# Hybrid SSD, attention and convolution trunk: the rows of ones of queries and keys come with a transfer, and a pool of tiles has 50 buffers instead of 52

## The chip, the cores and the metric

The kernel runs on one core of a Trainium2 chip. The metric is the time of one execution on the device in microseconds; lower is better. The core has a matrix engine (TensorE, PE in the profile, with its loads of the stationary operand as PEld), VectorE (DVE), ScalarE (ACT), GpSimd (POOL), and SyncE (SP), whose queue issues nearly all DMA transfers. Each engine executes its own list of instructions in order, and waits where an instruction needs another engine's result or a buffer that is still in use.

## The reference, cut to what matters

Two layers over 512 tokens of width 1024 in float32. The first has an input projection, 16 SSD heads, 16 heads of forgetting attention, and an output projection; the second is a gated convolution module. What bears on the change is the attention:

```python
c = jnp.cumsum(log_f, axis=1)
...
logits = jnp.einsum('bqhp,bkhp->bhqk', qi, k).astype(jnp.float32) * scale
logits = logits + jnp.transpose(cqi, (0, 2, 1))[..., None] - ck[:, :, None, :]
logits = jnp.where(kpos[None, :] <= qpos[:, None], logits, -jnp.inf)
w = jax.nn.softmax(logits, axis=-1).astype(v.dtype)
return jnp.einsum('bhqk,bkhp->bqhp', w, v)
```

To the product of query and key (64 elements each) the cumulated sum c of the query's token is added, and that of the key's token is subtracted.

## The kernel before, in words

All matrix products work on 32-bit values that are split into a high and a low part, each product being the sum of high times high, high times low and low times high. Weights come from memory as 512 KB pieces into the buffers `wr`, are split on ACT (high part) and on DVE or POOL (low part), and are used by a list of jobs (the class `Job`) in a fixed order; one job makes 128 columns of a projection. The low parts of some of the second layer's weights are made ahead, during the first layer: a piece is loaded (tile `pre`, line 202), its high part copied on ACT (line 211), the low part made on DVE (line 212), and stored to memory (line 216).

Beside the jobs, the class `Steps` deals out the work of the SSD heads and of the attention between a job's matmuls; a step is due when the steps that it needs are done for a stated number of microseconds of modelled TensorE time. TensorE's order is thus written out by hand. The other engines' order, and that of the transfers, is made by the compiler's list scheduler from priorities and modelled times.

Tiles come from pools. The pool `t` (line 54) holds tiles of 128 x 512 elements of 4 bytes; nearly all intermediate values live in it, among them `uh` and `ul` (the normed input, two parts), the four tiles of each attention head, the softmax's rows `pr`, the values `vhl`, and the sums `os`. A new tile of a full pool waits until an older one has been read for the last time.

The attention of a head h works on four tiles, which `qk_proj` makes when the projection of queries or keys is in PSUM (64 rows for each of two heads):

- `QS`: the high part of the query in rows 0 to 63 (ACT, line 610), the low part in rows 64 to 127 (DVE, line 611).
- `QX`: the high part again in rows 0 to 63 (a transfer from `QS`, line 612), and four more rows, 64 to 67: two of ones and two with the parts of the cumulated sum.
- `KS`: the high part of the key, twice (ACT, line 623, and a transfer, line 625).
- `KX`: the low part of the key in rows 0 to 63 (DVE, line 624), and four rows, 64 to 67: the two parts of the negative cumulated sum, and two of ones.

The logits of 128 queries (the step `sa`) are the matmul of QS with KS, that of the first 68 rows of QX with KX, and the mask. Then come the row maximum `nmx` on DVE (line 1503), the exponential into `pr` on ACT, the reciprocal of the row sum `ri` on DVE (line 1508), and the product of both on POOL (line 1509). In the step `sb` TensorE transposes `pr` into `pT`, and the transposed rows are split into `ph` and `pl`; the step `sc` multiplies them with the values.

The four additional rows come in two steps: POOL fills rows 64 to 67 with ones (lines 613 and 626), and a transfer from `chl` overwrites two of them (lines 614 and 627). The tile `chl` holds the cumulated sums: rows 32 to 47 of the 16 heads, as high part `csh` and low part `csl`, and the same, negated, in rows 64 to 79 (lines 1216 to 1220).

Of the kernel before, what the change touches and what calls it, by code (L numbers as in the profile page):

```python
# [9 lines left out]
F32R = mybir.dt.float32r  # L10
BF16 = mybir.dt.bfloat16
AF = mybir.ActivationFunctionType
ALU = mybir.AluOpType
# [3 lines left out]
S = 512  # L17
# [19 lines left out]
def trunk(  # L37
# [6 lines left out]
    nc = tc.nc  # L44
    V, G, A, T = nc.vector, nc.gpsimd, nc.scalar, nc.tensor
# [3 lines left out]
    cp = ctx.enter_context(tc.tile_pool(name="const", bufs=1))  # L49
# [1 line left out]
    ep = ctx.enter_context(tc.tile_pool(name="early", bufs=4))  # L51
    eh = ctx.enter_context(tc.tile_pool(name="earlyh", bufs=2))
    qp = ctx.enter_context(tc.tile_pool(name="q", bufs=7))
    tp = ctx.enter_context(tc.tile_pool(name="t", bufs=52))
    hp = ctx.enter_context(tc.tile_pool(name="spill", bufs=8, space=bass.MemoryType.DRAM))
    lop = ctx.enter_context(tc.tile_pool(name="los", bufs=64, space=bass.MemoryType.DRAM))
    sp = ctx.enter_context(tc.tile_pool(name="small", bufs=8))
# [15 lines left out]
    def t2(s, dt=F32):  # L73
        return tp.tile([P, S], dt, tag="t", name=nm(s))
# [10 lines left out]
    def f32(t):  # L85
        return t.bitcast(F32)
# [431 lines left out]
    def fm_job(w, c0, evac, uh, ul, eng=None):  # L518
        def go(wh, wl):
            pb = bank("m")  # L520
            yield from fm_chunks(pb, P, wh, wl, uh, ul)
            evac(pb)
        return Job(w, 0, KT, c0, P, go, eng)
# [80 lines left out]
    def qk_proj(j):  # L604
        def evac_q(pq):
            for s in range(2):
                h = 2 * j + s
                src = slice(64 * s, 64 * s + 64)
                QS, QX = t2("QS", F32R), t2("QX", F32R)
                A.mul(QS[0:64, :], pq[src, :], 0.125)  # L610
                V.scalar_tensor_tensor(QS[64:128, :], pq[src, :], 0.125, f32(QS)[0:64, :], ALU.mult, ALU.subtract)
                nc.sync.dma_start(f32(QX)[0:64, :], f32(QS)[0:64, :])
                G.memset(f32(QX)[64:68, :], 1.0)
                nc.sync.dma_start(f32(QX)[66:68, :], f32(chl)[32 + h : 33 + h, :, :])
                qk["q", h] = (QS, QX)
                done["q", h] = now[0]

        def evac_k(pk):
            for s in range(2):
                h = 2 * j + s  # L620
                src = slice(64 * s, 64 * s + 64)
                KS, KX = t2("KS", F32R), t2("KX", F32R)
                A.copy(KS[0:64, :], pk[src, :])
                V.tensor_tensor(KX[0:64, :], pk[src, :], f32(KS)[0:64, :], ALU.subtract)
                nc.sync.dma_start(f32(KS)[64:128, :], f32(KS)[0:64, :])
                G.memset(f32(KX)[64:68, :], 1.0)
                nc.sync.dma_start(f32(KX)[64:66, :], f32(chl)[64 + h : 65 + h, :, :])
                qk["k", h] = (KS, KX)
                done["k", h] = now[0]
        fm_job(e_w_in, C_Q + j * P, evac_q, uh, ul)  # L630
        fm_job(e_w_in, C_K + j * P, evac_k, uh, ul)
# [581 lines left out]
        V.tensor_tensor(stk[0:16, :], spl[0:16, :], ee[0:16, :], ALU.mult)  # L1213
        act(stk[96:112, :], cs[0:16, :], AF.Exp)

    chl = cp.tile([80, 2, S], F32R, name="chl")
    csh, csl = chl[:, 0, :], chl[:, 1, :]
    A.copy(csh[0:48, :], cs)
    V.tensor_tensor(csl[0:48, :], cs, f32(csh)[0:48, :], ALU.subtract)
    V.tensor_scalar(chl[64:80], f32(chl)[32:48], -1.0, None, ALU.mult)  # L1220

    cs2 = cp.tile([P, S], F32R, name="cs2")
    sel2 = cp.tile([P, 16], F32R, name="sel2")
# [423 lines left out]
```

## Time and profile before

| | before |
|---|---|
| median of 3 runs | 916.59 us (916.2 to 918.29) |
| the profiled execution | 917.41 us, its span 915.6 us |
| granted TensorE clock, mean | 0.994 |
| PE busy | 888.8 us (97%) |
| DVE busy | 711.5 us (78%) |
| ACT busy | 613.2 us (67%) |
| POOL busy | 508.7 us (56%) |
| moved by DMA | 170.32 MB |

All times inside an execution are counted from the start of its span. An engine's idle time is put down to the instruction that ended it, the releaser; `A <- B: 1.1, 1, 1.1` in a table of waits says that A waited for B for 1.1 us in total, once, the longest 1.1. In a list in order of time each row has start and duration in us, engine, line, operation and tiles, and in brackets the idle time just before it with its releaser. In the tables of stages each engine has its busy time and its number of instructions, and at the end stand the granted clock of TensorE, the mean busy share of the 16 DMA engines, and GB/s.

### The profile page before, as it was taken

The page shows a single profiled execution, that of the slowest core. Times are in us where ns is not written, and L with a number is a line of the kernel's source. Part 1 is how long each engine was busy: PE and PEld are TensorE (multiplying, and loading weights), DVE is VectorE, ACT ScalarE, POOL GpSimd, SP SyncE. Part 2 cuts the span into 40 slices and gives each one's busy share as a digit, 9 for nine tenths or more (in the row PEclk, how much of TensorE's full clock was granted, in tenths as well). Part 3 has the DMA queues.
Part 4 walks back from the last instruction along what each step waited for, and adds up shares of the span by engine and source line. Part 5 has one row for each costly group of instructions (what it writes and reads, how often), then busy time and mean ns, then how long its engine had stood idle before and what let it go on. Part 6 is the DMA issues. An engine that isn't in the chain of part 4 may idle for free. (4 is left out here: it accounts for less than half of the span.)

```text
span 915.6 us, 13920 instructions
## 1 busy us (share of the span) xinstructions
PE 888.8 (97%) x4603; PEld 747.9 (82%) x4603; DVE 711.5 (78%) x1270; ACT 613.2 (67%) x1159; POOL 508.7 (56%) x478
## 2 busy tenths in 40 slices
PE   6999999999999999999999999999999999999997
PEld 6888888887889888888678889888888887787885
DVE  5667959788975877869887258999999999889402
ACT  6767587677766776767775538787876959558300
POOL 2723665526443353344743214898999999747310
PEclk9999999999999999999999999999999999999999
DMA  7726523348775585865768993565574754544502
GB/s 211 234 78 216 157 74 88 98 155 256 240 254 174 174 278 163 264 211 173 251 209 301 328 356 103 163 190 155 185 221 149 226 184 146 177 140 159 184 11 104
DMA packets 185068, 170.32 MB, mean 186 GB/s; under 512 B 8413, under 2 KB 152421, under 8 KB 184997
## 3 DMA queue, kind: packets, MB, share of 16 engines
q1 hardware_dynamic: 184980, 169.44, 57.9%
q8 instruction: 36, 0.59, 0.3%
q14 instruction: 36, 0.29, 0.1%
q10 hardware_dynamic: 16, 0.00, 0.0%
HBM read 133.64 MB, written 31.46 MB: 180 GB/s over the span
## 5 line engine op out<-in xcount | busy, mean ns | idle before, releaser
L102 PE MATMUL m<-uh,w 128*128 128x512 f32 (+1 forms) x1392 | 450.8, 391 | 2.0 <-ACT yT L1441 0.8
L102 PEld LDWEIGHTS m<-uh,w 128*128 128x128 f32 x1392 | 260.3, 189 | 51.0 <-ACT yT L1441 1.2
L102 PE MATMUL m<-ul,w 128*128 128x512 f32 (+1 forms) x696 | 266.9, 384 | 0.0
L191 POOL TENSOR_TENSOR w<-wr,w 128x512 fp32r<-128x512 f32 x112 | 159.2, 1446 | 141.9 <-ACT w L159 104.6
L989 DVE SCALAR_TENSOR_TENSOR acc<-h,cw,acc 128x490 f32<-128x490 f32 (+13 forms) x274 | 178.8, 725 | 2.7 <-ACT acc L981 2.0
L896 POOL TENSOR_TENSOR acc<-acc,prod 128x507 f32<-128x507 f32 (+9 forms) x124 | 159.5, 1289 | 8.2 <-ACT prod L882 0.7
L102 PEld LDWEIGHTS m<-ul,w 128*128 128x128 f32 x696 | 131.7, 189 | 21.7 <-issue 0.5
L102 PE MATMUL o<-w,hlh 128*128 128x512 f32 x448 | 140.9, 396 | 0.0
L212 DVE TENSOR_TENSOR pre<-pre,prh 128x512 fp32r<-128x512 f32 x104 | 92.7, 916 | 23.9 <-ACT prh L211 23.1
L102 PEld LDWEIGHTS o<-w,hlh 128*128 128x128 f32 x448 | 82.9, 190 | 15.7
L102 PE MATMUL tm<-w,uh 128*128 128x256 f32 (+1 forms) x384 | 93.3, 334 | 0.0
L159 ACT CAST w<-wr 128x1024 fp32r<-128x1024 f32 x72 | 75.0, 1050 | 20.5 <-DMA wr<-in_e_w_in_dram 7.7
L102 PE MATMUL o<-w,hll 128*128 128x512 f32 x224 | 87.7, 392 | 0.0
L1509 POOL TENSOR_SCALAR pr<-pr,ri 128x128 f32<-128x128 f32 (+1 forms) x64 | 39.7, 621 | 85.6 <-DVE ri L1508 61.8
L882 ACT ACTIVATE prod<-h,cw 128x507 f32<-128x507 f32 (+9 forms) x124 | 79.0, 709 | 0.0
L211 ACT CAST prh<-pre 128x512 fp32r<-128x512 f32 x104 | 62.0, 622 | 16.8 <-DVE pre L212 14.8
L351 POOL TENSOR_TENSOR rstd<-var,mhalf 128x1 f32<-128x1 f32 (+1 forms) x20 | 12.9, 643 | 107.9 <-DVE var L349 83.0
L157 ACT CAST w<-wr 128x1024 fp32r<-128x1024 f32 x56 | 57.2, 1050 | 17.9 <-DMA wr<-in_o_w_out_dram 11.0
L102 PEld LDWEIGHTS tm<-w,uh 128*128 128x128 f32 x384 | 65.0, 196 | 4.7
L102 PE MATMUL tm<-w,ul 128*128 128x256 f32 (+1 forms) x192 | 62.2, 324 | 0.0
L95 ACT ACTIVATE pr<-s,nmx 128x128 f32<-128x128 f32 (+1 forms) x64 | 33.9, 530 | 37.1 <-DVE nmx L1503 21.2
L102 PEld LDWEIGHTS o<-w,hll 128*128 128x128 f32 x224 | 42.3, 189 | 9.1
(265 smaller groups left out, 1537.7 us busy)
## 6 DMA issues: line engine op xcount, KB each, us to landing
wr<-in_e_w_in_dram SPq DMA_DIRECT2D x56, 512.0 KB
lo<-pre SPq DMA_DIRECT2D x52, 512.0 KB
pre<-in_o_w_in_dram SPq DMA_DIRECT2D x48, 512.0 KB
wr<-in_o_w_in_dram SPq DMA_DIRECT2D x48, 512.0 KB
w<-lo SPq DMA_DIRECT2D x48, 512.0 KB
wr<-in_e_w_out_dram SPq DMA_DIRECT2D x16, 512.0 KB
wr<-in_o_w_out_dram SPq DMA_DIRECT2D x16, 512.0 KB
x<-in_x_dram SPq DMA_DIRECT2D x12, 256.0 KB
```

Of the source, the lines that this page charges most:

```text
L95: i = A.activation(*a, **kw)
L102: T.matmul(o, l, r, start=start, stop=stop, skip_group_check=True)
L157: last_cast[0] = A.copy(hi, src).ins
L159: last_cast[0] = A.copy(hi, src).ins
L191: j.eng.tensor_tensor(hl[1][i][:, sl], src[:, sl], f32(hl[0][i])[:, sl], ALU.subtract)
L211: A.copy(h, t[:, sl])
L212: V.tensor_tensor(t.bitcast(F32R)[:, sl], t[:, sl], f32(h), ALU.subtract)
L351: mark["rstd"] = G.tensor_tensor(r, v, mhalf.to_broadcast([P, ss.shape[-1]]), ALU.pow).ins
L882: A.activation(prs[i][:, s:], hs[j][:, : S - s], AF.Copy, scale=w31(30 - s, j))
L896: G.tensor_tensor(a2[j][:, s:], a2[j][:, s:], prs.pop(i)[:, s:], ALU.add)
L989: V.scalar_tensor_tensor(a[:, s:], h[:, : S - s], w31(30 - s, j), a[:, s:], ALU.mult, ALU.add)
L1509: G.tensor_scalar(p[:, :L], p[:, :L], ri, 1.0, ALU.mult, ALU.mult)
```

## The change

The tile `chl` gets two more rows of 512 for each partition, so that it is 80 x 4 x 512. POOL fills it with ones once. The parts of the cumulated sums stand in its rows 2 and 3 in partitions 0 to 47, the negated ones in rows 0 and 1 of partitions 64 to 79. Partition 32 + h thus holds ones, ones, high, low, and partition 64 + h negative high, negative low, ones, ones. One transfer brings all four rows to QX or KX, and the 32 memsets of rows 64 to 67 are gone. The four kilobytes that `chl` needs more in each partition are two buffers of the pool `t`.

```diff
-    tp = ctx.enter_context(tc.tile_pool(name="t", bufs=52))
+    tp = ctx.enter_context(tc.tile_pool(name="t", bufs=50))
...
                 nc.sync.dma_start(f32(QX)[0:64, :], f32(QS)[0:64, :])
-                G.memset(f32(QX)[64:68, :], 1.0)
-                nc.sync.dma_start(f32(QX)[66:68, :], f32(chl)[32 + h : 33 + h, :, :])
+                nc.sync.dma_start(f32(QX)[64:68, :], f32(chl)[32 + h : 33 + h, :, :])
...
                 nc.sync.dma_start(f32(KS)[64:128, :], f32(KS)[0:64, :])
-                G.memset(f32(KX)[64:68, :], 1.0)
-                nc.sync.dma_start(f32(KX)[64:66, :], f32(chl)[64 + h : 65 + h, :, :])
+                nc.sync.dma_start(f32(KX)[64:68, :], f32(chl)[64 + h : 65 + h, :, :])
...
-    chl = cp.tile([80, 2, S], F32R, name="chl")
-    csh, csl = chl[:, 0, :], chl[:, 1, :]
+    chl = cp.tile([80, 4, S], F32R, name="chl")
+    G.memset(f32(chl), 1.0)
+    csh, csl = chl[:, 2, :], chl[:, 3, :]
     A.copy(csh[0:48, :], cs)
     V.tensor_tensor(csl[0:48, :], cs, f32(csh)[0:48, :], ALU.subtract)
-    V.tensor_scalar(chl[64:80], f32(chl)[32:48], -1.0, None, ALU.mult)
+    V.tensor_scalar(chl[64:80, 0:2], f32(chl)[32:48, 2:4], -1.0, None, ALU.mult)
```

## The prediction

> **What bounds the kernel now.** I read the page's first part, then stages of the span, then who TensorE waited for, then the changed tiles. In the page each engine has its busy time, share and instructions:
>
> ```profile
> span 915.6 us, 13920 instructions
> PE 888.8 (97%) x4603; PEld 747.9 (82%) x4603; DVE 711.5 (78%) x1270; ACT 613.2 (67%) x1159; POOL 508.7 (56%) x478
> ```
>
> TensorE (PE) is busy for 888.8 of 915.6 us, so an edit that takes no matmul away can win at most the 26.8 us of idle time, plus what a lowered clock costs. Where these lie is in the busy time by stage (us of the stage; its length, then PE, PEld, DVE, ACT, POOL; granted clock; DMA share):
>
> ```profile
> 0.00:28.00 28.00, 18.60 (x125) 17.00 (x125) 15.93 (x39) 17.21 (x39) 9.29 (x29) 1.00 0.68 199
> 100.00:260.00 160.00, 155.40 (x846) 133.73 (x845) 137.23 (x244) 114.05 (x206) 83.91 (x61) 0.98 0.51 156
> 248.00:256.00 8.00, 8.00 (x44) 8.00 (x43) 8.00 (x15) 5.12 (x10) 2.64 (x3) 0.57 0.56 178
> 260.00:390.00 130.00, 130.00 (x795) 111.12 (x794) 98.38 (x201) 91.17 (x211) 54.53 (x75) 1.00 0.70 217
> 390.00:400.00 10.00, 8.63 (x68) 7.80 (x67) 7.70 (x18) 5.94 (x17) 5.61 (x8) 1.00 0.62 177
> 436.00:440.00 4.00, 1.72 (x8) 0.89 (x8) 3.21 (x8) 1.82 (x5) 1.38 (x4) 0.99 1.00 340
> 440.00:444.00 4.00, 4.00 (x15) 3.12 (x15) 2.72 (x10) 2.74 (x10) 2.39 (x5) 0.58 0.59 234
> 444.00:480.00 36.00, 34.73 (x187) 27.48 (x186) 29.27 (x55) 29.09 (x62) 23.20 (x24) 1.00 0.67 216
> 480.00:820.00 340.00, 339.98 (x1607) 283.78 (x1606) 288.89 (x504) 238.31 (x421) 247.69 (x211) 1.00 0.62 204
> 820.00:840.00 20.00, 18.48 (x80) 14.68 (x79) 20.00 (x31) 16.10 (x26) 11.30 (x7) 1.00 0.38 131
> 909.30:915.60 6.30, 0.01 (x1) 0.00 (x0) 2.17 (x4) 0.69 (x2) 0.55 (x1) 0.90 0.22 85
> ```
>
> 9.4 us are idle before 28 us and 6.3 after 909.3, at the two ends. The heads of queries and keys, which the change touches, run from 260 to about 480 us; there PE stands still for 1.37 us (390 to 400), 2.28 (436 to 440) and 1.27 (444 to 480), 4.9 us together. Two stretches run at a lower clock though PE is busy in all of them: 8 us at 0.57, worth 8 x 0.43 = 3.4 us, and 4 us at 0.58, worth 1.7 us. Each follows idle time; the second stands right behind the 2.28 us. The whole stage thus holds 4.9 + 1.7 = 6.6 us that could be won. Whom PE waited for in it, in us, times, longest (the two ranges 380 to 400 and 420 to 440):
>
> ```profile
> PE pT L106 <- POOL pr L1509: 1.1, 1, 1.1
> PE pT L106 <- ACT pr L95: 1.3, 1, 1.3
> PE s L102 <- ACT pr L95: 1.0, 1, 1.0
> ```
>
> All three are steps of the softmax, none is QX or KX or a transfer.
>
> **The change part by part.** The changed tiles first (duration ns min/median/max, first and last start), then what SyncE's queue waited for POOL:
>
> ```profile
> L613 POOL MEMSET QX<- x16: 518/520/523, 268.2 to 428.0; 4x512 f32 x16
> L612 SPq DMA_DIRECT2D QX<-QS x16: 469/510/1562, 268.9 to 431.2; - x16
> L614 SPq DMA_DIRECT2D QX<-chl x16: 606/629/681, 269.4 to 431.8; - x16
> L626 POOL MEMSET KX<- x16: 518/519/522, 269.2 to 444.1; 4x512 f32 x16
> L627 SPq DMA_DIRECT2D KX<-chl x16: 593/628/669, 273.5 to 445.7; - x16
> L102 PE MATMUL s<-KX,QX x64: 270/309/400, 279.8 to 461.3; 68*128 68x128 f32 x16, 68*128 68x256 f32 x16, 68*128 68x384 f32 x16, 68*128 68x512 f32 x16
> ...
> SPq L627 <- POOL KX L626: 9.8, 6, 3.8
> SPq L614 <- POOL QX L613: 8.0, 5, 2.0
> ```
>
> *32 memsets go.* 16 x 0.520 + 16 x 0.519 = 16.6 us of POOL. POOL is busy 54.53 of 130 us in 260 to 390, and PE's one wait for POOL there is for pr, which itself waits for the reciprocal on DVE. Worth 0 on the path; what hides it is PE, busy for all of the 130 us.
>
> *32 transfers no longer wait for POOL.* SyncE's queue loses 9.8 + 8.0 = 17.8 us of waiting. Behind the waiting instruction stand the loads of weights and of the pieces for the second layer, and the stores of the low parts. PE waits for none of these between 260 and 480, so they come earlier for nothing: 0. Late next is the tile itself: a transfer that opens QX or KX must still wait for a free buffer, now on SyncE instead of POOL.
>
> *The transfers carry four rows instead of two.* 32 x 4 KB more is nothing beside 170 MB. The time to issue one: two rows take 0.63, 64 rows 0.51 us, so four lie at 0.51 to 0.68 (the longest of the two-row ones). I take 0.63, nearest in rows: 32 issues stay at 20.1 us of the queue. From the first of these transfers (269.4) to the first matmul on it (279.8) are 10.4 us, for keys 6.3 (273.5); a transfer that is later by its whole issue time is still in time. 0.
>
> *chl doubles and gets a memset.* 80 x 2048 elements on POOL. The start as it is (start, us, then idle time before it):
>
> ```profile
> 2.53 0.52 POOL L442 MEMSET keep<- 48x512 f32 x1
> 3.60 0.52 POOL L1224 MEMSET cs<- 128x512 f32 x1
> 5.49 0.56 POOL L351 TENSOR_TENSOR rstd<-var,mhalf 128x1 f32<-128x1 f32 x1 [1.34 <-DVE var L349]
> 7.67 0.56 POOL L351 TENSOR_TENSOR rstd<-var,mhalf 128x1 f32<-128x1 f32 x1 [1.62 <-DVE var L349]
> 20.96 1.05 ACT L159 CAST w<-wr 128x1024 fp32r<-128x1024 f32 x1 [3.81 <-DMA wr<-in_e_w_in_dram]
> 23.70 0.36 PE L102 MATMUL m<-uh,w 128*128 128x256 f32 x1 [0.71 <-DVE bm L502]
> ```
>
> 512 elements take 0.52 us whatever the partitions (48 x 512 of keep as well as 128 x 512 of cs), so 2048 take 4 x 0.52 = 2.1 us. The memset of cs stands late in the program and runs at 3.60, where POOL is free; the new one needs as little and will run there too. Then the first rstd starts at about 4.1 + 2.1 = 6.2 instead of 5.49, at most 0.7 us late; the second, at 7.67 behind 1.62 us of idle time, moves by a few tenths. This ends at 20.96: ACT waits 3.81 us there for a weight's transfer, and PE stands 0.71 us before the matmuls fed by it, so the start is set by that transfer. Bounds 0 and +0.7; I take 0, since 0.71 covers the larger. The three other operations on chl keep their sizes, and the first of them follows the scan that makes the cumulated sums, long after the memset.
>
> *Two buffers fewer in the pool t (52 to 50).* This is the one part that takes something from the path. Rows that show the pool at its limit:
>
> ```profile
> 331.24 0.52 POOL L613 MEMSET QX<- 4x512 f32 x1 [2.77 <-DVE QS L611]
> 380.42 0.52 POOL L613 MEMSET QX<- 4x512 f32 x1 [3.47 <-DVE QS L611]
> L1509 POOL TENSOR_SCALAR pr<-pr,ri x64: 374/588/1685, 281.3 to 465.1; 128x128 f32<-128x128 f32 x16, 128x256 f32<-128x256 f32 x16, 128x384 f32<-128x384 f32 x16, 128x512 f32<-128x512 f32 x16
> L588 ACT CAST vhl<-tm x16: 363/378/405, 256.4 to 404.0; 128x256 fp32r<-128x256 f32 x16
> ```
>
> These memsets read nothing and write a fresh tile, yet POOL stands idle 2.77 and 3.47 us for them: they wait until a buffer comes free. How much lead two buffers are: QS, QX, KS and KX make 64 tiles, pr 64, vhl 16, in all 144 from 268 to 465 us, one every 1.37 us. Two buffers are an estimated 2.7 us of lead, wherever the pool is full. KX has 6.3 us of lead and QX 10.4, which covers it; pr is the thin one, since PE already waits for it in 390 to 400 at the end of the full stretch. Lower end 0 (PE idles nowhere in the 130 us in which the two rows lie, with the pool full), upper end +2.7, since a PE that is held back by the lead lost gets that lead back. Tiles that open later also make engines execute in another order (only PE's is written out), which can be worth something of either sign; its bounds are the rivals. I take +0.3, near the lower end, because the 2.77 and 3.47 us of waiting left no mark on PE.
>
> **Sum.** 0 + 0 + 0 + 0 + 0.3. The profiled execution took 917.41 us around its span of 915.6, 0.8 above the median of the runs, 916.59. 917.41 + 0.3 = 917.7 against that execution, 916.6 + 0.3 = 916.9 against the median, which is the forecast.
>
> **Rivals.** *Slower: the pool's loss lands on PE.* Place: 385 to 400 us, where pT waits for pr. It decides if a pr tile's start is put off by more than what is left before its transpose. Price +2.7, so 919.3; if the new stall brings a stretch of low clock, another 1.7 to 3.4, so 921.0 to 922.7. For it: the two slot waits, and PE's wait for pr. Against: 130.00 of 130 in the stage where they lie. [...]
>
> *Faster: the stall at 436 us and the low clock behind it go.* What makes it now:
>
> ```profile
> 432.77 4.08 DVE L212 TENSOR_TENSOR pre<-pre,prh 128x512 fp32r<-128x512 f32 x3
> 436.96 0.42 DVE L1503 TENSOR_REDUCE nmx<-s 128x1 f32<-128x256 f32 x1
> 433.12 3.19 POOL L119 TENSOR_TENSOR hll<-yT,hlh 128x512 fp32r<-128x512 f32 x2 [4.59 <-PE o L102]
> ```
>
> Three subtractions for the second layer run on DVE at 1.36 us each beside a POOL that subtracts too, and the row maximum that PE needs waits behind them. With transfers that reach SyncE earlier, the pieces of those subtractions come at other times; if they leave this place, 2.28 + 1.7 = 4.0 us go: 912.6. With the 1.37 us of 390 to 400 as well, 911.2. Against: the last QX memsets are over 4 us before, so nothing removed stands in this chain.
>
> *The start:* the new memset not hidden, +0.7: 917.3, inside no change.
>
> *The change doesn't do what it says:* SyncE waits for the free buffer for as long as it waited for POOL (the 2.77 and 3.47 us are such waits). 916.6, the same class.
>
> **How the numbers follow.** The forecast with the last two rivals 0.44, the slower one 0.31, the faster one 0.25. A measurement of this kernel can tell about 0.2%, 1.8 us: same is 914.8 to 918.4, the forecast's own range. For 8 in 10 the range takes in the faster rival's 912.6 and the slower one with the smaller dip, 921.0; outside are the double gain and the larger dip.
>
> **What the profile after would show.** Right: no QX or KX memset on POOL, one of about 2.1 us on chl at 3 to 6 us; no wait of the transfers from chl for POOL; QX and KX in time; PE busy 888 to 889 us, 260 to 390 without idle time, and the stalls at 390 to 400 and 436 to 440 about as now. Slower: new waits of pT for pr between 300 and 400, a clock under 0.9 behind them. Faster: 440 to 444 at full clock. Wrong altogether: if the stages from 480 on, or those before 260, changed; DVE, ACT and POOL could be ordered anew there too, and the 3.4 us of low clock at 248 could move, for which I have no row.

## The result, and the profile after

The changed kernel takes 921.77 us (median of 8 runs, 919.25 to 923.83) and the kernel before 917.44 us (8 runs, 915.34 to 919.24). The ratio is 1.0050, with a 95% interval of 1.0035 to 1.0066: slower by 4.3 us. The forecast was 916.9 with a range of 912.6 to 921.0.

The profiled execution took 921.53 us. The first part of its page:

```profile
span 919.8 us, 13860 instructions
PE 890.5 (97%) x4603; PEld 748.8 (81%) x4603; DVE 708.7 (77%) x1270; ACT 613.6 (67%) x1159; POOL 497.0 (54%) x447
```

POOL lost 11.7 us of work (508.7 before): 16.6 us of memsets are gone, the one on `chl` brings 1.8, and its other work takes 3.1 us longer. The span grew by 4.2 us. The same table of stages as before (length, then PE, PEld, DVE, ACT, POOL; granted clock; DMA share; GB/s):

```profile
248.00:256.00 8.00, 8.00 (x55) 8.00 (x56) 8.00 (x14) 5.22 (x9) 2.56 (x3) 0.79 0.55 167
260.00:320.00 60.00, 60.00 (x353) 51.05 (x353) 42.64 (x88) 40.96 (x95) 17.52 (x22) 1.00 0.70 215
320.00:390.00 70.00, 65.23 (x391) 54.97 (x389) 50.55 (x103) 46.63 (x105) 23.30 (x27) 0.98 0.65 202
390.00:400.00 10.00, 8.96 (x74) 8.29 (x72) 7.86 (x20) 7.15 (x20) 5.83 (x7) 1.00 0.68 222
400.00:440.00 40.00, 40.00 (x234) 33.26 (x233) 31.54 (x61) 29.53 (x64) 14.62 (x17) 1.00 0.63 201
440.00:446.00 6.00, 4.13 (x21) 2.64 (x20) 5.01 (x12) 2.88 (x9) 1.77 (x5) 1.00 1.03 353
446.00:450.00 4.00, 4.00 (x16) 3.20 (x15) 2.80 (x9) 2.86 (x9) 1.50 (x3) 0.57 0.11 31
450.00:480.00 30.00, 29.40 (x161) 23.03 (x160) 23.25 (x46) 24.54 (x55) 22.98 (x22) 1.00 0.64 205
480.00:820.00 340.00, 339.98 (x1607) 283.75 (x1606) 288.89 (x504) 238.22 (x420) 244.07 (x210) 1.00 0.63 207
```

From 320 to 390, where PE had no idle time before, it is now idle for 70 - 65.23 = 4.77 us. From 260 to 480 it stands still for 4.77 + 1.04 + 1.87 + 0.60 = 8.3 us, against 4.9 before. From 480 to 820 nothing changed. Since TensorE's order is the same in both kernels, the start of each of its 4603 matmuls can be set against the start of the same matmul before: the lag is +0.07 us at 240, -1.27 at 260 (less low clock at 248), still -1.27 at 320, +5.23 at 350, +4.55 from 480 to 820. The loss of 6.5 us lies between 320 and 350: two waits of 2.75 and 1.84 us, shown below, and an estimated 1.7 us for 3.41 us at half clock behind the second, from 343.61 us. Against it stand 1.3 us won at 248 us, where this execution ran for 3.4 us at half clock and the one before for 6.8, and 0.7 us after 350.

Who PE waited for between 300 and 480 us (in total, times, longest):

```profile
PE pT L106 <- POOL pr L1508: 5.6, 3, 2.7
PE s L102 <- ACT pr L95: 1.0, 1, 1.0
PE pT L106 <- ACT pr L95: 0.9, 2, 0.6
```

The transposes wait for pr on POOL, 5.6 us instead of 1.1. The third of these waits, 1.04 us at 396.77, is as long as the one that was there before. The first, from the lists of DVE, ACT (two rows), POOL (two rows) and PE of the changed kernel:

```profile
319.52 0.69 DVE L1502 TENSOR_REDUCE nmx<-s 128x1 f32<-128x512 f32 x1
321.94 2.00 ACT L159 CAST w<-wr 128x1024 fp32r<-128x1024 f32 x2 [0.33 <-PE o L102]
323.96 0.69 ACT L95 ACTIVATE pr<-s,nmx 128x512 f32<-128x512 f32 x1
323.07 3.51 POOL L191 TENSOR_TENSOR w<-wr,w 128x512 fp32r<-128x512 f32 x2 [2.79 <-ACT w L159]
326.56 1.74 POOL L1508 TENSOR_SCALAR pr<-pr,ri 128x512 f32<-128x512 f32 x1
328.35 0.66 PE L106 MATMUL pT<-ident,pr 128*128 128x128 f32 x4 [2.75 <-POOL pr L1508]
```

and the same place in the kernel before:

```profile
322.56 0.69 ACT L95 ACTIVATE pr<-s,nmx 128x512 f32<-128x512 f32 x1
323.24 1.98 ACT L159 CAST w<-wr 128x1024 fp32r<-128x1024 f32 x2
323.69 0.70 POOL L1509 TENSOR_SCALAR pr<-pr,ri 128x512 f32<-128x512 f32 x1 [1.82 <-issue]
324.36 3.54 POOL L191 TENSOR_TENSOR w<-wr,w 128x512 fp32r<-128x512 f32 x2
326.72 0.60 PE L106 MATMUL pT<-ident,pr 128*128 128x128 f32 x4
```

Two engines changed their order. Before, ACT makes the exponential and then casts two weights; POOL scales pr (0.70 us) and then splits the weights (3.54 us). After, the row maximum is ready at 320.21, but ACT casts the weights first and begins the exponential at 323.96, 3.75 us later. POOL, which gets the cast weights first, splits them first, and pr stands behind 3.51 us of that. PE waits 2.75 us. By the program's tiles and the trace, the buffer of this pr was one that a transpose had just given back at 322.9. This step is a reconstruction: the runs below test the size of the pool and ACT's order, and not this buffer.

At 343 us it happens again (DVE, ACT in three rows, POOL in two, PE):

```profile
334.44 0.42 DVE L1502 TENSOR_REDUCE nmx<-s 128x1 f32<-128x256 f32 x1
336.50 0.48 ACT L95 ACTIVATE pr<-s,nmx 128x256 f32<-128x256 f32 x1 [2.53 <-PE o L102]
338.96 1.05 ACT L159 CAST w<-wr 128x1024 fp32r<-128x1024 f32 x1
339.90 0.69 ACT L95 ACTIVATE pr<-s,nmx 128x512 f32<-128x512 f32 x1
340.09 2.51 POOL L191 TENSOR_TENSOR w<-wr,w 128x512 fp32r<-128x512 f32 x2 [0.65 <-ACT w L159]
342.58 1.03 POOL L1508 TENSOR_SCALAR pr<-pr,ri 128x512 f32<-128x512 f32 x2
343.32 0.89 PE L106 MATMUL pT<-ident,pr 128*128 128x128 f32 x4 [1.84 <-POOL pr L1508]
```

In the kernel before, at this place, pr is scaled first and the cast follows (POOL, then ACT):

```profile
337.95 1.19 POOL L1509 TENSOR_SCALAR pr<-pr,ri 128x512 f32<-128x512 f32 x1 [1.16 <-DVE ri L1508]
339.15 1.05 ACT L159 CAST w<-wr 128x1024 fp32r<-128x1024 f32 x1
```

The exponential at 336.50 is how a wait for a buffer looks. It reads s and nmx, which are ready at 334.44 + 0.42 = 334.86, and ACT goes on standing idle for 1.64 us more, until a matmul o is done, which is none of its inputs. Of what that matmul reads, the program keeps only vhl in the pool t, so a buffer of vhl is the likely one that pr needed.

### The profile page after: what moved, and what is told of

Read it like the earlier page. It is cut to its first block, busy times and chain, and to the rows that moved or that the text cites. A ratio compares the mean times of both kernels' runs of the same rounds, so it can differ in the third digit from the quotient of the medians.

```text
span 919.8 us, 13860 instructions
## 1 busy us (share of the span) xinstructions
PE 890.5 (97%) x4603; PEld 748.8 (81%) x4603; DVE 708.7 (77%) x1270; ACT 613.6 (67%) x1159; POOL 497.0 (54%) x447
## 4 chain that ended last, share of the span: by engine, by line
PE 48%; DVE 2%; ACT 1%; issue 1%; DVEq 0%; POOLq 0%; ACTq 0%
PE m L102 28%; PE o L102 17%; PE acc L102 1%; PE uT L106 0%; DVE cvo L1085 0%; DVE cvo L1086 0%; PE pT L106 0%; DVE ws L191 0%; DVE pl L119 0%; PE s L102 0%; PE st L102 0%; DVE nmx L1502 0%; DVEq L1641 0%; ACT pr L95 0%; DVE w L191 0%
## 5 line engine op out<-in xcount | busy, mean ns | idle before, releaser
L191 POOL TENSOR_TENSOR w<-wr,w 128x512 fp32r<-128x512 f32 x112 | 161.7, 1470 | 151.7 <-ACT w L159 92.7
L157 ACT CAST w<-wr 128x1024 fp32r<-128x1024 f32 x56 | 57.2, 1049 | 18.4 <-DMA wr<-in_o_w_out_dram 10.4
```

Of the source, the lines that this page charges most:

```text
L157: last_cast[0] = A.copy(hi, src).ins
L191: j.eng.tensor_tensor(hl[1][i][:, sl], src[:, sl], f32(hl[0][i])[:, sl], ALU.subtract)
```

## The experiments

All were timed in turn with the kernel before on the same chip; each experiment has 6 to 12 runs. The row of the kernel before joins its runs beside the three sets of experiments (at full clock 910.1, 910.4 and 910.2, so that the sets can be compared), and the change's own eight runs were beside another eight (917.44). One execution's time has two parts that can be told apart: its span times its mean granted clock is an estimate of what the span would have been at full clock, and the rest is lost to lowered clock. Both are means over all runs of a kernel; the standard error is 0.1 to 0.2 us for the kernel before, and 0.2 to 0.8 us for the others. The lost part also counts the half clock behind the last matmul, which costs nothing and is 0.6 us in the profiled execution before and 1.4 in that of the change, so differences of under 1 us say little.

| kernel | buffers in t | median, us | ratio to before (95%) | at full clock | lost to clock |
|---|---|---|---|---|---|
| before (94 runs) | 52 | 917.1, 917.0, 917.4 | 1 | 910.2 | 5.1 |
| the change | 50 | 921.77 | 1.0050 (1.0035 to 1.0066) | 914.3 | 5.6 |
| e1 pool alone | 50 | 922.18 | 1.0055 (1.0038 to 1.0072) | 913.3 | 6.9 |
| e2 pool alone | 51 | 918.44 | 1.0012 (0.9998 to 1.0027) | 912.4 | 4.2 |
| e3 rows from memory | 52 | 914.39 | 0.9976 (0.9963 to 0.9988) | 909.5 | 3.4 |
| e4 rows from memory | 54 | 914.58 | 0.9979 (0.9965 to 0.9994) | 909.1 | 4.1 |
| e10 rows from memory | 51 | 917.70 | 1.0004 (0.9987 to 1.0022) | 911.5 | 4.4 |
| e8 rows from memory | 50 | 923.04 | 1.0063 (1.0039 to 1.0087) | 913.4 | 7.8 |
| e6 e3, memsets waited for | 52 | 915.54 | 0.9993 (0.9978 to 1.0009) | 909.0 | 5.0 |
| e7 e3, memsets not waited for | 52 | 916.32 | 0.9985 (0.9969 to 1.0002) | 909.3 | 5.1 |
| e5 the change, ACT's order | 50 | 919.92 | 1.0030 (1.0012 to 1.0047) | 913.8 | 4.3 |
| e9 the change, order from job 38 | 50 | 919.14 | 1.0018 (1.0000 to 1.0037) | 912.2 | 5.4 |
| e11 e4, order from job 38 | 54 | 913.98 | 0.9957 (0.9942 to 0.9973) | 908.5 | 3.8 |
| e12 e4, pr in its own pool | 48 + 6 | 919.22 | 1.0012 (0.9997 to 1.0026) | 910.4 | 6.3 |

**The smaller pool alone (e1, e2).** The kernel before with one number changed:

```diff
-    tp = ctx.enter_context(tc.tile_pool(name="t", bufs=52))
+    tp = ctx.enter_context(tc.tile_pool(name="t", bufs=50))     # e1; 51 in e2
```

> The kernel before with 50 buffers in the pool t instead of 52, and nothing else: memsets and transfers as before. Theory A (the two buffers are the cost): 3 to 5 us slower than before, with new waits of pT for pr between 300 and 400 us. Theory B (the cost is in the transfers without memsets, which reach SyncE in another order): within 1.5 us of before. Theory C (every new order of the engines is worth some us of either sign, whatever is changed): anything within 4 us of before, either side.

> The kernel before with 51 buffers. Theory A: between before and the kernel with 50, 1 to 3 us slower than before. Theory B: within 1.5 us. Theory C: no order between 50, 51 and 52; it may be the slowest or the fastest of the three.

e1 is as slow as the whole change, a little above the 3 to 5 us of theory A. Its waits of PE between 300 and 400 us, and POOL's list at the place of the first:

```profile
PE pT L106 <- POOL pr L1509: 4.7, 2, 2.8
```

```profile
323.78 3.51 POOL L191 TENSOR_TENSOR w<-wr,w 128x512 fp32r<-128x512 f32 x2 [2.83 <-issue]
327.26 1.75 POOL L1509 TENSOR_SCALAR pr<-pr,ri 128x512 f32<-128x512 f32 x1
```

The order is turned round as in the changed kernel, with the memsets in place and chl at its old size. With 51 buffers POOL's list shows the old order again, and PE waits for no pr on POOL between 300 and 400:

```profile
321.47 0.70 POOL L1509 TENSOR_SCALAR pr<-pr,ri 128x512 f32<-128x512 f32 x1 [1.85 <-DVE ri L1508]
322.13 3.52 POOL L191 TENSOR_TENSOR w<-wr,w 128x512 fp32r<-128x512 f32 x2
```

The median of e2 stands only 1.4 us above before, which fits theory A and theory B and looks like an edge between 51 and 50. At full clock it is none: 910.2, 912.4, 913.3. In e2 less was lost to the clock.

**The rest of the change without the smaller pool (e3, e4, e8, e10).** The four rows of each head come from a tile in device memory, written once, so that chl takes no room and 50 to 54 buffers fit. The memsets are gone as in the change.

```diff
+    chp = ctx.enter_context(tc.tile_pool(name="chd", bufs=1, space=bass.MemoryType.DRAM))
...
-                G.memset(f32(QX)[64:68, :], 1.0)
-                nc.sync.dma_start(f32(QX)[66:68, :], f32(chl)[32 + h : 33 + h, :, :])
+                nc.sync.dma_start(f32(QX)[64:68, :], chd[h, 0:4, :])
...
+    csh, csl, neg, onr = row("csh", F32R), row("csl", F32R), [row("nh"), row("nl")], row("onr")
...
+    chd = chp.tile([16, 8, S], F32, name="chd")
+    for r, src in enumerate((onr, onr, f32(csh), f32(csl), neg[0], neg[1], onr, onr)):
+        nc.sync.dma_start(chd[:, r, :], src[32:48, :])
```

> The four rows of QX and KX come in one transfer as in the change, but from a tile in DRAM (16 heads x 8 rows) that is written once, so that chl takes no SBUF and the pool t keeps 52 buffers. Theory A: no slower than before, 916 to 918 us, no wait of pT for pr over 1.5 us between 300 and 390. Theory B: 3 to 5 us slower, as the change. Theory C: within 4 us, either side.

> The same with 54 buffers, which the SBUF freed by chl holds. Theory A: the fastest of the four, 1 to 4 us faster than before, since the stall at 390 to 400 us goes with the shortage. Theory B: 3 to 5 us slower than before. Theory C: within 4 us, either side, and not ordered with 52.

> The kernel with the four rows from DRAM, with 50 buffers instead of 52. Pool theory: 3 to 6 us more than with 52, 917.5 to 920.5, with the waits of pT for pr between 300 and 350 us again. If the shortage costs only together with the memsets or with the transfers from SBUF: within 1.5 us of 914.4.

> The four rows from DRAM with 51 buffers, between 52 (914.39) and 50 (923.04). Pool theory with a cost that grows with each buffer: 917 to 920. Pool theory with an edge (a buffer costs nothing until an exponential is overtaken): within 1.5 us of 914.4, as 51 was near 52 in the kernel before.

With 52 buffers it beats the kernel before by 0.24%, more than theory A of e3 allowed; 54 is not the fastest, as theory A of e4 had it. With 50 the loss is back, and so are the three waits; its median lies above its band, with 7.8 us lost to the clock. e10 lies in the band of a cost that grows with each buffer. PE's waits for pr between 300 and 400, in e3 and then in e8:

```profile
PE pT L107 <- POOL pr L1512: 0.3, 1, 0.3
```

```profile
PE pT L107 <- POOL pr L1512: 5.6, 3, 2.8
```

At full clock 54, 52, 51 and 50 buffers give 909.1, 909.5, 911.5 and 913.4: nothing to win above 52, and some 2 us for each buffer below it. Both series together (e1 and e2 with the memsets, these without) say that the pool alone makes the change slower. The 0.7 us between before and e3 at full clock, if they are more than chance, aren't the memsets: with these back (e6, e7) they stay.

**The memsets by themselves (e6, e7).** e3 with the 32 memsets put back: in e6 on the rows that the transfer overwrites, so that it waits; in e7 on rows 96 to 99, which nothing reads, so that the transfer of the four rows needn't wait. In the traces these transfers wait 17.5 us for the memsets in e6 and 0.5 in e7.

```diff
+                G.memset(f32(QX)[64:68, :], 1.0)      # e6; rows 96:100 in e7; the same for KX
                 nc.sync.dma_start(f32(QX)[64:68, :], chd[h, 0:4, :])
```

> The kernel with the four rows from DRAM and 52 buffers (914.39), with the 32 memsets back in their place: POOL writes rows 64 to 67 and the transfer overwrites them, so it waits for POOL again. If POOL's time or the transfers' waiting is what those 2.7 us came from: 916.5 to 918.5. If they came from something else (the place of the new steps, the clock, another order): 914 to 915.5.

> The same, but the 32 memsets write rows 96 to 99 of the same tiles, which nothing reads: POOL spends the same 16.6 us in the same places, and no transfer waits for it. Theory P (POOL's time): 916.5 to 918.5, as with the memsets in their place. Theory W (the transfers' waits for POOL): 914 to 915.5, as without memsets.

At full clock they cost nothing that shows: 909.0 and 909.3 against 909.5. Their medians are 1.2 and 1.9 us above e3, and that lies in the clock (5.0 and 5.1 lost against 3.4). Whether the memsets cause this or the runs fell that way isn't settled, with standard errors of 0.5 to 0.7. The wait and POOL's time can't be told apart either: the two intervals overlap, and both medians lie between the bands or at their edge.

**ACT's order (e5, e9).** The changed kernel, and a cast of weights may not overtake an exponential that stands before it in the program, in e5 from job 32 on, in e9 from job 38:

```diff
-        if done:
+        if 32 <= state["run"] < JO + 3 and last_table[0] is not None:     # 38 in e9
+            with tc.issue_after(last_table[0]):
+                last_cast[0] = A.copy(hi, src).ins
+        elif done:
```

> The changed kernel (50 buffers), with one rule of order more: in the stage of the attention ACT's casts of weights may not be issued ahead of an exponential that the program writes before them. Theory A1 (the late buffer lets the casts overtake the exponential, POOL's subtraction for the weight then stands ahead of pr, and that makes the stall): the 2.75 us stall near 328 us falls under 1 us, and the time to 916 to 920. Theory A2 (the late buffer alone makes it): the stall stays over 2 us, 921 to 923. The rule can cost something of its own, where a cast waits for an exponential that waits for a buffer: new waits of PE for w.

> The changed kernel with the rule of order only from job 38 on, so that the casts at the first heads are free and the 3.5 us wait for the transfer of KS near 279 us should go, while the rule holds at 320 to 345 us. Theory A1 (the order of casts and exponentials carries the cost of the smaller pool): 917 to 918.5, no stall over 1.5 us between 300 and 390. Theory A2 (the late buffers cost by themselves): 920 or more.

As the `elif` shows, the rule also takes the place of an older one in these jobs, by which a cast waits for a read-out of PSUM some jobs before; the two are not tested apart. In both runs the stalls of 2.75 and 1.84 us are gone. Between 300 and 400 PE waits for pr, and now also for pl, as the first rows below say, which are the same in both. POOL's list of e9 at the place shows pr ahead of the split, after a wait of 5.40 us:

```profile
PE pT L106 <- DVE pl L119: 1.2, 1, 1.2
PE pT L106 <- POOL pr L1511: 0.9, 2, 0.6
PE s L102 <- DVE pl L119: 0.9, 1, 0.9
```

```profile
323.45 0.69 POOL L1511 TENSOR_SCALAR pr<-pr,ri 128x512 f32<-128x512 f32 x1 [5.40 <-DVE ri L1510]
324.11 2.55 POOL L194 TENSOR_TENSOR w<-wr,w 128x512 fp32r<-128x512 f32 x2
```

The gain is smaller than the 4.6 us of stalls. In e5 the rule makes a stall of its own earlier, where a transfer of KS comes late, with a clock of 0.63 behind it (PE's waits over the span, then a stage):

```profile
PE s L102 <- DMA KS<-KS: 3.5, 1, 3.5
```

```profile
279.00:287.00 8.00, 8.00 (x35) 6.47 (x36) 2.27 (x7) 3.02 (x8) 1.44 (x3) 0.63 0.86 276
```

e9 hasn't got that stall; its 919.14 lies between the bands of A1 and A2. At full clock it wins 2.0 us (914.26 - 912.23) of the 4.1 that the change cost, about half. The turned order thus carries about half of the price. That the other half is the late buffers isn't shown by e9, since its waits for pl can be the rule's own: e11, with the rule and 54 buffers, has them too (2.0 and 1.0 us from 260 to 480). The kernels with 51 buffers say more. They have the old order and not the rule, cost 2.2 (e2) and 2.0 us (e10 against e3) at full clock, and between 320 and 390 PE stands idle for 1.17 and 1.06 us, where it had no idle time with 52 (e2, then e10):

```profile
320.00:390.00 70.00, 68.83 (x438) 58.81 (x437) 55.86 (x112) 50.38 (x117) 30.91 (x41) 1.00 0.73 226
```

```profile
320.00:390.00 70.00, 68.94 (x422) 58.09 (x421) 56.29 (x113) 48.95 (x112) 24.90 (x30) 1.00 0.71 224
```

So a missing buffer costs something before any order turns.

**Both together (e11), and a pool of its own for pr (e12).** e11 is e4 with the order rule of e9. e12 is e4 with its 54 buffers divided, 48 for t and 6 for pr alone.

```diff
-    tp = ctx.enter_context(tc.tile_pool(name="t", bufs=54))
+    tp = ctx.enter_context(tc.tile_pool(name="t", bufs=48))
+    prp = ctx.enter_context(tc.tile_pool(name="pr", bufs=6))
...
-                p = pr[h, i] = t2("pr")
+                p = pr[h, i] = prp.tile([P, S], F32, tag="pr", name=nm("pr"))
```

> The four rows from DRAM, 54 buffers, and the rule of order from job 38 on. With 54 buffers no exponential should be overtaken, so by A1 the rule has little to mend: 913 to 916. If it still holds back casts, new waits of PE for w: 916 to 918.

> The four rows from DRAM and 54 buffers, of which 6 are a pool of their own for pr, so that no other tile can hold one of them. If the exponential's buffer is still late somewhere with 54: 912 to 914. If six fixed buffers hold pr back or starve the rest (48): 916 to 920, with waits of PE for pr.

e11 has the best ratio, 0.9957, and beats both kernels; its interval overlaps those of e3 and e4. In e12 PE waits for nothing from 320 to 400 (it is busy for 70.00 of 70 us from 320 to 390), but it waits longer at an earlier place, 4.0 us from 240 to 260 against 1.7 in the kernel before:

```profile
PE yd L104 <- DVE H L1350: 2.6, 1, 2.6
PE yd L104 <- DVE hll L121: 1.4, 1, 1.4
```

At full clock e12 is 1.3 us slower than e4, and the clock took another 2.2 us. That the waits at 240 us come from the smaller rest of the pool (48 instead of 54) is likely, since little else differs, but no row shows such a wait. In this division, six buffers for pr alone were worth less than the same six for all.

## Why the prediction was wrong, step by step

- *What bounds the kernel; the stages before 240 us and from 480 to 820 unchanged:* right. The lag is 0.07 us at 240 and constant from 480 to 820. Two readings are loose: PE's wait for POOL that is put into 260 to 390 lies at 394.96, and the idle time of 444 to 480 is for pl on DVE (0.94 and 0.25 us), which the list of waits leaves out. Neither carries the forecast.
- *32 memsets go, worth 0:* right at full clock (e3 against e6 and e7), with 1 to 2 us of clock open.
- *SyncE's 17.8 us of waits, worth 0; late next is the free buffer:* right. SyncE's queue of the changed kernel waits at the same transfers for other things, 2.1 us of it still for POOL, at pr. The longest waits for others are (in total, times, longest):

```profile
SPq L613 <- PE pT L106: 2.7, 2, 2.3
SPq L625 <- PE o L102: 1.5, 1, 1.5
```

  Neither a transpose nor a matmul o makes anything that these transfers read; so these are most likely waits until a buffer comes free.
- *Four rows at 0.63 us each, in time:* right. PE waited for no QX, KX or transfer from chl. The medians are 0.638 us for QX and 0.646 for KX.
- *The memset of chl, 2.1 us at 3.6, hidden:* right. It took 1.80 us, less than the 2.1 that four times 0.52 make. The first rstd came 0.13 us earlier than before, and the second, at 7.73, 0.06 later; the memset of cs went behind the first:

```profile
3.59 1.80 POOL L1215 MEMSET chl<- 80x2048 f32 x1
5.36 0.55 POOL L351 TENSOR_TENSOR rstd<-var,mhalf 128x1 f32<-128x1 f32 x1
```

- *Two buffers fewer, bounds 0 to +2.7, taken at +0.3 "because the 2.77 and 3.47 us of waiting left no mark on PE":* this is the step that failed. The two buffers cost 3.2 us in e1, 3.9 from e3 to e8, and 4.1 in the change itself, all at full clock. The mechanism was named, and the upper end of 2.7 us was not far off, but the lower end was taken on a wrong argument. The two memsets that wait belong to QX, which by the prediction's own rows had 10.4 us of lead. That they leave no mark says something of QX and nothing of pr. The number to look up was the slack of pr itself, and it stood in the trace: at the place above, pr ended at 323.69 + 0.70 = 324.39, and its transpose began at 326.72, 2.33 us later. That is less than the 2.7 us of lead that the prediction had just reckoned, in a stretch where the pool is full. At the second place it was only 0.56 us (339.14 to 339.70). Slack under the lead tells that a loss is possible and not where it falls: set in order against the transposes, 12 of the 41 pr that POOL scales before 400 us had less than 2.7 us, and in the changed kernel PE waits for three.
- *Tiles that open later make engines execute in another order, "of either sign":* the rival's price was made from the lead alone. The order was about half of the loss (e9). At the first place the instruction that came ahead is long: 3.51 us against a slack of 2.33.
- *The slower rival:* its mechanism is what happened, its place (385 to 400 us) was late by some 50 us, and with a dip of the clock it was priced 921.0 to 922.7, which holds the 921.77. It had 0.31 and the forecast 0.44. That the number fits is partly luck: the rival made it of 2.7 us of waiting and 1.7 to 3.4 of clock, and the runs make it of 4.1 us at full clock and 0.5 of clock.
- *"If the new stall brings a stretch of low clock, another 1.7 to 3.4":* there is one, right behind the second stall, 8 x 0.21 = 1.7 us:

```profile
340.00:348.00 8.00, 6.16 (x39) 5.65 (x38) 4.95 (x14) 4.90 (x14) 4.00 (x5) 0.79 0.51 144
```

  Over all runs the change lost only 0.5 us more to the clock than before, e1 1.8 us.
- *The base of 916.6:* the median of three runs of the kernel before; its eight runs beside the change gave 917.44. Of the 4.9 us between forecast and measurement 0.8 are this.
- *The faster rival:* the stall at 436 us didn't go. It is 1.87 us at 440 to 446 with a clock of 0.57 behind it.
- *"PE idles nowhere in the 130 us", the lower end of 0:* with 50 buffers the trace has gaps on PE, of 2.75 and 1.84 us. With 52 there was no gap from 260 to 390, and yet no buffer to spare (e2 and e10, some 2 us for one). Here the absence of gaps didn't mean slack.

Left open: pr took 1.74 us instead of 0.70 behind the split at 326.56 (1.75 in e1), which is 1 us of the first stall. While it ran, DVE made this subtraction, whose two inputs both lie in SBUF:

```profile
327.14 0.67 DVE L212 TENSOR_TENSOR pre<-pre,prh 128x512 fp32r<-128x512 f32 x1
```

In the trace before and in the one after, each pr that takes over 0.3 us longer than others of its shape (8 and 7 of 64) runs beside such an operation of DVE on two tiles in SBUF for 0.49 us or more; no other pr does so for more than 0.29 us. No run takes these operations away, so that they are the cause isn't shown. It also stays open what the change itself costs with 51 or 52 buffers; it wasn't run, since the larger chl takes their room.

## What to carry to other kernels

Before two buffers are given away, set the lead that they are (buffers times the time between two new tiles) against the slack of the thinnest tile of that pool, read as the time from the end of its last writer to the start of its reader; a wait of another tile says nothing of it. A slack under the lead is a warning, and a run with fewer buffers and nothing else changed (e1) settles it. Under a list scheduler a tile that is ready a little late can lose its turn to a long instruction (here one of 3.51 us, against a slack of 2.33), so the loss can be that instruction's length and not the delay. Small constant rows can be staged in device memory: here that removed the same memsets, with as many transfers to QX and KX, and took no room from the pool (e3, ratio 0.9976).

## What the runs showed of the hardware

In the traces before and after the low clock comes in pieces. The granted clock in their records is 0.5 or 1.0, and the low stretches are 3.41 us long (from 248.04, 343.61 and 446.01 us in the change, from 439.93 before) or 6.83 us, twice that (from 248.78 before), apart from the last one of each trace, which begins behind the last matmul and runs into the end. In e8 the granted clock from 246 to 260 us (0.69 in 3 us, 0.50 in 7, 0.83 in 4) lost 5.1 us, an estimated 10.2 us at half. PE waits for H ahead of 248 us for 1.35 us before, 1.31 in the change, 1.32 in e8 and 1.34 in e3, and what follows is 6.83, 3.41, an estimated 10.2 and, in e3, no us of low clock, though the change doesn't touch that place. The stage 248 to 256 was 0.57 before and 0.79 after; in e8 and in e3 it is

```profile
248.00:256.00 8.00, 8.00 (x37) 8.00 (x38) 8.00 (x14) 5.25 (x9) 2.57 (x3) 0.50 0.51 164
```

```profile
248.00:256.00 8.00, 8.00 (x69) 8.00 (x70) 8.00 (x15) 5.11 (x9) 2.62 (x3) 1.00 0.55 166
```

A piece of 3.41 us at half clock costs an estimated 1.7 us. The lag shows 1.5 for the one that the change has less at this place (+0.26 at 247, -1.27 at 256). By the estimate this one place makes 0 to 5 us of difference between these four executions, as much as the whole change. Executions of one kernel differ too: the mean granted clock of the 94 of the kernel before goes from 0.990 to 0.998. The prediction priced this place at 3.4 us from one execution. Why the same wait is followed by more or less low clock is not shown by any run here. Nor does the length of the idle time alone decide it: in the trace of the change the wait of 1.84 us that ended at 343.32 was followed by half clock, and the longer one of 2.75 us that ended at 328.35 by full clock (1.00 from 320 to 330).
